# Operands of a TensorE-bound encoder layer, moved by 64 to 128 bytes within a partition

## The chip, the cores and the metric

The kernel runs on one core of a Trainium2 chip. The metric is the device time of one execution in microseconds (us), as the median of several runs. The profile is one further execution.

## The reference

One layer of an encoder block is applied to two requests, of 256 and of 512 tokens, with the same weights; the model width is 1024. Cut to what matters:

```python
h = rmsnorm(x, norm_mix_g)
u, q, k, v, qm, gl = split(h @ w_in)
s5_out   = z * sigmoid(z @ s5_w_glu)          # z = gelu(scan of u, both directions)
diff_out = diff_attention(q, k, v)            # 8 heads, two softmax maps each
mem_out  = memory_attention(qm, rmsnorm(mem)) # 4 heads, 256 memory tokens
br       = [s5_out, diff_out, mem_out] @ w_branch
merged   = sum(sigmoid(gl + b_gate) * br)
x        = x + merged @ w_out
g, up    = split(rmsnorm(x) @ w_gate_up)      # 2 x 2816 columns
x        = x + (silu(g) * up) @ w_down
```

## The kernel before

The two requests are laid side by side as 768 tokens, in two segments (`SEGS`) of 256 and 512. Activations are held feature-major, as tiles of 128 partitions by 8 blocks by 768 tokens.

Each float32 operand is split into a rounded high part and the rest, both of type fp32r, and each product of two operands is three products on TensorE (`mm3`, L755): high by high, high by low, low by high. These three are the lines L756, L757 and L758 of the profile.

```python
def mm3(ps, wh, wl, xh, xl, start, stop):
    pe.matmul(ps, wh, xh, start=start, stop=False)
    pe.matmul(ps, wh, xl, start=False, stop=False)
    pe.matmul(ps, wl, xh, start=False, stop=stop)
```

The first operand of a product is stationary (the weights of TensorE), the second streams. Two helpers call `mm3` over 8 blocks of contraction. `dense_fm` (L760) keeps a weight of the network stationary and streams a segment of an activation, so 256 or 512 columns; `dense_tm` (L766) keeps 128 tokens of an activation stationary and streams columns of the network's weight. In the page's names `gl<-Hhi,wh` the streamed operand stands first.

The order of the work: memory attention (tiles mk, mv, mq, ms, mo), the scan's input (u), the gates (gl, interleaved with the scan), query and key (qk), values (v) and the attention of the eight heads, the branch on the memory attention (br on xm), the half-GLU (glu on z), the branches on the scan (br on s5o) and on the attention (br on xd), the output projection (wo, on mgd), and the FFN. `WStream` loads every weight of the network in order through three buffers, splits it on ScalarE and VectorE (or by DMA) and keeps four pairs of parts ahead.

The FFN goes over the 2816 columns in 11 blocks of 256. The first block multiplies f directly (`first`); each of the ten later ones (`block`, L1389) uses a scheme with seven products of halves instead of eight, 384 columns wide, whose right factors are parts of f (B11, B12 and so on) and the sums T1, T2, T3 in a pool `ffT`; T4 is written over B12. Then `down` (L1423) multiplies the hidden part, tile hid in pool `ffh`, stationary, by two blocks of `w_down`, 512 columns at a time. For `w_down` the first of the two blocks lies in extra tiles (`W.extra`, pools `wxh` and `wxl`), the second in the ordinary ones.

Tiles live in pools that are opened and closed like a stack, from the low end of the partition ("left") or from its high end ("right"). One right-hand pool H holds the normalised input; when it is closed, pool XA takes its place and holds xm, then s5o, then mgd. On the left, pool XB holds z, then xd, then f; after it come x1 (the residual), the FFN's pools, the extra weight tiles, `wsum`, `ffT` and `ffh`. These addresses are fixed when the program is built.

Of the kernel before, what the change touches and what calls it, by code (L numbers as in the profile page):

```python
# [8 lines left out]
F32 = mybir.dt.float32  # L9
# [619 lines left out]
def hybrid_block(ctx, tc, A, outs, consts):  # L629
# [20 lines left out]
    def uid(s):  # L650
        cnt[0] += 1
        return f"{s}_{cnt[0]}"
# [74 lines left out]
            W.add(cols("w_gate_up", 256 * fb + (DFF if what == "up" else 0)), 8, 256, "w" if fb else None)  # L727


    def rsqrt(x, n, tag, bufs=4):  # L730

        i = sm.tile([128, n], I32, name=uid("rqi"), tag=f"rqi{n}")
        y = sm.tile([128, n], F32, name=uid("rqy"), tag=tag, bufs=bufs)
        t = sm.tile([128, n], F32, name=uid("rqt"), tag=f"rqt{n}")
        v.tensor_scalar(out=i, in0=x.bitcast(I32), scalar1=1, scalar2=None, op0=ALU.logical_shift_right)
        v.tensor_scalar(out=y.bitcast(I32), in0=i, scalar1=-1.0, scalar2=float(0x5F3759DF), op0=mul, op1=add)
        for _ in range(3):
            v.tensor_tensor(out=t, in0=y, in1=y, op=mul)
            v.scalar_tensor_tensor(out=t, in0=t, scalar=-0.5, in1=x, op0=mul, op1=mul)
            v.scalar_tensor_tensor(out=y, in0=t, scalar=1.5, in1=y, op0=add, op1=mul)  # L740
        return y
# [78 lines left out]


    hctx, qctx, mctx = ExitStack(), ExitStack(), ExitStack()
    hp_ = hctx.enter_context(tc.tile_pool(name="H", bufs=1, side="right"))
    H = tuple(hp_.tile([128, 8, TOK], F32R, name=f"H{w}") for w in ("hi", "lo"))
    k1 = qctx.enter_context(tc.tile_pool(name="ma1", bufs=1, side="right"))
# [13 lines left out]
    def mem_units(h):  # L839
# [11 lines left out]
        w = W.get()  # L851
        mean_eps(ss, 4, 256)
        rs = rsqrt(ss, 4, "krs")
        for tt in range(4):
            v.scalar_tensor_tensor(out=kr[:, tt], in0=kr[:, tt], scalar=rs[:, tt : tt + 1], in1=gk,
# [32 lines left out]
    def mem_attend():  # L888

        for h in range(4):  # L890
# [9 lines left out]
            qs = sm.tile([128, TILES], F32, name=uid("qs"), tag="qs")  # L900
            v.tensor_scalar(out=qs, in0=ps[:, 0:TILES], scalar1=1.0 / 256, scalar2=1e-6, op0=mul, op1=add)
            rq = rsqrt(qs, TILES, "rq")
            yield
            P, PT = {}, {}
# [51 lines left out]
    with tc.tile_pool(name="nrm", bufs=1) as pool, tc.tile_pool(name="nrmg", bufs=1) as pg:  # L956
# [10 lines left out]
        for tt in range(4):  # L967
# [5 lines left out]
            square_sum(xm[tt], pool, mss[:, tt : tt + 1])  # L973
        mean_eps(mss, 4, 1024)
        v.tensor_copy(mrs, rsqrt(mss, 4, "krs"))
        g = bcast_load(pg, A["norm_mix_g"][0], 1024, "gmix")
        xr = [load_rows(pool, xs[tt]) for tt in range(TILES)]
# [95 lines left out]
    x1ctx, dctx, wctx = ExitStack(), ExitStack(), ExitStack()  # L1073
# [362 lines left out]
    with ExitStack() as c5:  # L1436
# [6 lines left out]
        def pair(pool, nm):  # L1443
            return tuple(pool.tile([128, 8, TOK], F32R, name=uid(nm + w), tag="X" + w) for w in ("hi", "lo"))
# [29 lines left out]
        def load_pair(X, src, scale=None, more=()):  # L1474
            for m in range(8):
                p = zst if m in more else stg
                r = p.tile([128, TOK], F32, name=uid("brr"), tag="brr")
                gp.dma_start(r, src[m])
                split_evac(X[0][:, m], X[1][:, m], r, scale)
# [8 lines left out]
        def tail(c):  # L1488
            if c != 3:
                return  # L1490
            dat.drain()
            dctx.close()
            L["XB"] = x1ctx.enter_context(tc.tile_pool(name="XB", bufs=1))
            Z = L["Z"] = pair(L["XB"], "z")
            load_pair(Z, z_scr, 0.5, (2, 3, 4, 7))
            zctx.close()
            xp = x1ctx.enter_context(tc.tile_pool(name="x1", bufs=1))
            L["x1"] = [xp.tile([128, 1024], F32, name=f"x1_{t}") for t in range(TILES)]

        branch(2, Xm, first=True, tick=dat.tick, hook=tail)  # L1500
        x1, XB, Z = L["x1"], L["XB"], L["Z"]
        S = pair(XA, "s5o")
# [27 lines left out]
        c6 = ctx.enter_context(ExitStack())  # L1530
# [56 lines left out]

    W.extra = tuple(c6.enter_context(tc.tile_pool(name="wx" + w, bufs=1)) for w in "hl")
    W.sums = c6.enter_context(tc.tile_pool(name="wsum", bufs=3))
    tp = c6.enter_context(tc.tile_pool(name="ffT", bufs=1))  # L1590
    fh = c6.enter_context(tc.tile_pool(name="ffh", bufs=1))

    B = {f"B{k}{t}": tuple(x[:, 4 * k - 4 : 4 * k, HT * t - HT : HT * t] for x in F)
# [102 lines left out]
```

## Time and profile before

| | us |
|---|---|
| median of 3 runs | 1806.25 (1805.45 to 1807.45) |
| the profiled execution | 1807.31 |
| its span | 1805.5 |
| PE busy (products) | 1773.6 |
| PEld busy (weight loads, beside the products) | 1629.6 |
| DVE, ACT, POOL busy | 1287.0, 881.7, 278.9 |

The span runs from the first to the last instruction that the profiler saw; the time of the execution is 1.8 us longer. A product's record in the profile is longer than the distance to the start of the next, since products are pipelined; what PE spends on one is read from start to start.

### The profile page before, as it was taken

What the parts mean: (1) busy time and instruction counts of PE and PEld (TensorE: products, weight loads), DVE (VectorE), ACT (ScalarE), POOL (GpSimd) and SP (SyncE); (2) the same over time, 40 slices, a digit from 0 to 9 for tenths busy, and PEclk for the clock granted to TensorE, in tenths of its full rate; (3) what the DMA queues carried; (4) which work ended last, traced back from release to release, by engine and by line L of the source; (5) the groups of instructions that cost most, each with busy time, mean ns of one, the idle gap of its engine ahead of it and who ended that gap; (6) DMA issues with size and microseconds to landing.
All of it is one profiled execution on the core that took longest, in us unless ns stands there. A gap on an engine that the chain in (4) does not pass through costs nothing.

```text
span 1805.5 us, 29484 instructions
## 1 busy us (share of the span) xinstructions
PE 1773.6 (98%) x11286; PEld 1629.6 (90%) x11286; DVE 1287.0 (71%) x2375; ACT 881.7 (49%) x1852; POOL 278.9 (15%) x300
## 2 busy tenths in 40 slices
PE   7999999999999999999989999999999999999999
PEld 7999988999999999999969888888889999999997
DVE  6555758799999568778875535442689777777775
ACT  7444544777676357777656434232333333333331
POOL 0000000000000101111020101000115333333330
PEclk9999999999999999999999999999999999999999
DMA  8422646564655587443373535322302222222221
GB/s 264 128 93 96 112 130 164 145 150 124 155 144 151 143 194 189 112 112 89 88 216 105 199 119 177 105 100 82 82 24 94 71 70 71 71 71 71 71 70 70
DMA packets 192300, 213.12 MB, mean 118 GB/s; under 512 B 58144, under 2 KB 161824, under 8 KB 192160
## 3 DMA queue, kind: packets, MB, share of 16 engines
q1 hardware_dynamic: 174656, 147.27, 27.1%
q0 software_dynamic: 16352, 60.83, 14.5%
q10 hardware_dynamic: 1152, 3.15, 0.5%
q8 instruction: 89, 1.46, 0.3%
q14 instruction: 51, 0.42, 0.1%
HBM read 146.11 MB, written 32.57 MB: 99 GB/s over the span
## 4 chain that ended last, share of the span: by engine, by line
PE 56%; DVE 5%; DMA 4%; ACT 2%; issue 1%; SPq 1%; POOL 0%; ACTq 0%; DVEq 0%; POOLq 0%
PE br L757 4%; PE br L758 4%; PE br L756 4%; PE dn L756 3%; PE dn L757 3%; PE dn L758 3%; PE gate L756 3%; PE gate L757 3%; PE gate L758 3%; PE up L756 3%; PE up L758 3%; PE up L757 3%; PE av L1261 2%; PE qk L758 2%; PE qk L757 2%; PE qk L756 2%
## 5 line engine op out<-in xcount | busy, mean ns | idle before, releaser
L597 ACT ACTIVATE wh<-wr 128x1024 fp32r<-128x1024 f32 x146 | 164.4, 1127 | 98.8 <-DMA wr<-in_w_down_dram 20.1
L603 DVE TENSOR_TENSOR wl<-wr,wh 128x1024 fp32r<-128x1024 f32 x90 | 118.8, 1320 | 91.8 <-ACT wh L597 91.5
L601 POOL DMA_DIRECT2D wl<-wr x56 | 48.9, 873 | 562.3 <-ACT wl L600 466.5
L756 PE MATMUL gl<-Hhi,wh 128*128 128x256 f32 (+1 forms) x384 | 133.1, 347 | 0.8 <-ACT glt L1065 0.8
L757 PE MATMUL gl<-Hlo,wh 128*128 128x256 f32 (+1 forms) x384 | 129.9, 338 | 0.0
L758 PE MATMUL gl<-Hhi,wl 128*128 128x256 f32 (+1 forms) x384 | 129.8, 338 | 0.0
L1431 DVE TENSOR_TENSOR x<-x,dn 128x512 f32<-128x512 f32 x132 | 88.9, 685 | 57.2 <-PE dn L758 57.1
L756 PE MATMUL qk<-wh,Hhi 128*128 128x256 f32 x384 | 108.8, 283 | 1.1 <-ACT qksq L1131 1.1
L757 PE MATMUL qk<-wl,Hhi 128*128 128x256 f32 x384 | 108.7, 283 | 0.0
L758 PE MATMUL qk<-wh,Hlo 128*128 128x256 f32 x384 | 108.6, 283 | 0.0
L559 ACT ACTIVATE wh_S<-ws 128x512 fp32r<-128x512 f32 x70 | 41.7, 623 | 130.5 <-PE dn L758 103.8
L756 PE MATMUL dn<-wh,hidh 128*128 128x512 f32 x264 | 102.4, 390 | 1.2 <-DVE x L1431 1.0
L757 PE MATMUL dn<-wl,hidh 128*128 128x512 f32 x264 | 102.9, 390 | 0.0
L758 PE MATMUL dn<-wh,hidl 128*128 128x512 f32 x264 | 100.8, 390 | 0.0
L756 PEld LDWEIGHTS gl<-Hhi,wh 128*128 128x128 f32 x384 | 72.4, 188 | 8.7 <-ACT glt L1065 1.0
L758 PEld LDWEIGHTS gl<-Hhi,wl 128*128 128x128 f32 x384 | 72.3, 188 | 8.7
L757 PEld LDWEIGHTS gl<-Hlo,wh 128*128 128x128 f32 x384 | 72.4, 188 | 7.8
L756 PEld LDWEIGHTS qk<-wh,Hhi 128*128 128x128 f32 x384 | 72.9, 190 | 2.0 <-ACT qksq L1131 1.3
L758 PEld LDWEIGHTS qk<-wh,Hlo 128*128 128x128 f32 x384 | 73.1, 190 | 0.6
L757 PEld LDWEIGHTS qk<-wl,Hhi 128*128 128x128 f32 x384 | 72.9, 190 | 0.6
L1230 DVE TENSOR_REDUCE nm<-sc 128x1 f32<-128x512 f32 (+1 forms) x96 | 56.8, 597 | 22.5 <-PE sc L1225 21.6
L1232 ACT ACTIVATE p<-sc,nm 128x512 f32<-128x512 f32 (+1 forms) x96 | 59.0, 618 | 24.6 <-DVE nm L1230 20.1
(455 smaller groups left out, 5954.0 us busy)
## 6 DMA issues: line engine op xcount, KB each, us to landing
wl<-wr POOLq DMA_DIRECT2D x56, 512.0 KB, 5.2
wr<-in_w_in_dram SPq DMA_DIRECT2D x48, 512.0 KB, 4.7
wr<-in_w_gate_up_dram SPq DMA_DIRECT2D x44, 512.0 KB, 3.4
wr<-in_w_branch_dram SPq DMA_DIRECT2D x24, 512.0 KB, 4.1
wr<-in_w_down_dram SPq DMA_DIRECT2D x22, 512.0 KB, 3.8
glr<-gl_scr POOLq DMA_DIRECT2D x24, 384.0 KB, 3.4
wr<-in_w_mem_kv_dram SPq DMA_DIRECT2D x16, 512.0 KB, 5.1
wr<-in_w_in_dram SPq DMA_DIRECT2D x32, 256.0 KB, 4.3
```

What stands on the lines that cost most here:

```text
L559: self.nc.scalar.activation(f(hi), src, AF.Copy)
L597: self.nc.scalar.activation(hi, r, AF.Copy)
L601: self.nc.gpsimd.dma_start(lo, r.bitcast(F32R), accum_op=ALU.add)
L603: self.sub.tensor_tensor(out=lo, in0=r, in1=hi.bitcast(F32), op=ALU.subtract)
L756: pe.matmul(ps, wh, xh, start=start, stop=False)
L757: pe.matmul(ps, wh, xl, start=False, stop=False)
L758: pe.matmul(ps, wl, xh, start=False, stop=stop)
L1230: v.tensor_reduce(out=nm[:, m : m + 1], in_=ps, axis=AX.X, op=ALU.max, negate=True)
L1232: act.activation(pm[:, 0:n], ps, AF.Exp, bias=nm[:, m : m + 1], accum_out=s1s[:, tt : tt + 1] if m == 0 else s2)
L1261: pe.matmul(po[:, 0:128], aT[:, 128 * k : 128 * k + 128], V[:, c0 // 128 + k, 128 * (h % 2) : 128 * (h % 2) + 128], start=(k == 0), stop=( ...
L1431: v.tensor_tensor(out=o, in0=o, in1=ps, op=add)
```

## The change

A helper opens a pool with one tile of `n` bytes per partition that nothing uses, so that the pools that are opened after it on the same side start `n` bytes further in. It is called four times: 96 bytes on the right ahead of H, 64 on the left ahead of XB, and 128 each ahead of `ffT` and of `ffh`.

```diff
+    def offset(c, side, n):
+
+        p = c.enter_context(tc.tile_pool(name=uid("offset"), bufs=1, side=side))
+        p.tile([128, n // 4], F32, name=uid("pad"))
...
     hctx, qctx, mctx = ExitStack(), ExitStack(), ExitStack()
+    offset(ctx, "right", 96)
     hp_ = hctx.enter_context(tc.tile_pool(name="H", bufs=1, side="right"))
...
             dctx.close()
+            offset(x1ctx, "left", 64)
             L["XB"] = x1ctx.enter_context(tc.tile_pool(name="XB", bufs=1))
...
     W.sums = c6.enter_context(tc.tile_pool(name="wsum", bufs=3))
+    offset(c6, "left", 128)
     tp = c6.enter_context(tc.tile_pool(name="ffT", bufs=1))
+    offset(c6, "left", 128)
     fh = c6.enter_context(tc.tile_pool(name="ffh", bufs=1))
```

Each engine has the same instructions in the same order, with the same waits, before and after. What differs is where the tiles start in the partition:

| tiles (pool) | start before | start after | modulo 256, before | after |
|---|---|---|---|---|
| weights' parts wh, wl (`whi`, `wlo`) | 25856 and up | the same | 0 | 0 |
| H; later xm, s5o, mgd (`H`, `XA`) | 180192 | 180096 | 224 | 128 |
| memT, kT, V of the memory (`ma0`, `ma2`) | 106432 and up | 96 less | 192 | 96 |
| z, xd, f (`XB`) | 67840 | 67904 | 0 | 64 |
| extra weight tiles (`wxh`, `wxl`) | 151808 and up | 64 more | 0 | 64 |
| T1, T2, T3 (`ffT`) | 166144 and up | 192 more | 0 | 192 |
| hid (`ffh`) | 203008 | 203328 | 0 | 64 |
| attention's tiles (`da1`, `da2`), the scan's (`s5p`, `s5q`) | | the same | | |

Within a tile, parts lie at multiples of 512 bytes from its start, so that the start fixes the remainder for all of them.

## The prediction

> **What bounds the kernel.** I read the head of the page first, then the waits of PE, then the busy time of every engine by stage, and last some stretches in which PE does one kind of product and nothing else.
>
> ```profile
> span 1805.5 us, 29484 instructions
> PE 1773.6 (98%) x11286; PEld 1629.6 (90%) x11286; DVE 1287.0 (71%) x2375; ACT 881.7 (49%) x1852; POOL 278.9 (15%) x300
> ...
> PEclk9999999999999999999999999999999999999999
> ```
>
> PE is busy for 98% of the span at a full clock (a 9 stands for 90% or more). What PE waits for is small; these are the longest rows of its waits, and the whole list is 23 rows long and falls to 0.2 us.
>
> ```profile
> PE qkT L1177 <- DVE qst L1187: 3.9, 2, 2.9
> PE mv L756 <- ACT kr L847: 3.3, 2, 2.0
> PE nT L785 <- DVE memTlo L750: 1.9, 1, 1.9
> ```
>
> By stage (the second number behind the stretch is PE's busy time):
>
> ```profile
> core 0: us, PE busy (x) PEld busy (x) DVE busy (x) ACT busy (x) POOL busy (x), PEclk, DMA share, GB/s
> 7.92:301.67 293.75, 286.02 (x2003) 263.39 (x2003) 186.60 (x526) 152.10 (x286) 8.37 (x35) 1.00 0.50 132
> 301.67:616.15 314.48, 313.72 (x2156) 287.48 (x2154) 281.94 (x387) 212.54 (x489) 23.98 (x29) 1.00 0.58 149
> 616.15:1018.75 402.60, 389.07 (x2953) 368.79 (x2952) 290.26 (x719) 260.78 (x671) 46.20 (x71) 0.99 0.53 137
> 1018.75:1288.69 269.94, 269.94 (x1457) 232.58 (x1456) 121.72 (x176) 85.63 (x118) 20.47 (x39) 1.00 0.38 125
> ...
> 1389.61:1799.10 409.49, 409.28 (x2139) 380.91 (x2139) 314.53 (x443) 126.86 (x221) 146.05 (x101) 1.00 0.21 68
> ```
>
> From 1018.75 to the end PE practically never stops, and no other engine is near its length (DVE 314.53 of 409.49 us in the FFN). So a nanosecond on each product goes into the time one for one, and so does a nanosecond off it, until DVE is the bound, which is 95 us away in the FFN.
>
> **What a product costs, by width and by phase.** The change moves no instruction; it moves addresses. I call the start of an operand modulo 256 bytes its phase; the table in the section on the kernel lists the phases. PE reads two operands at once: the streamed (moving) one of a product, and the weights (stationary) of the next. What matters here is the time from start to start. The stretches below run from the first start of a run of one kind to the start of what follows, so length over number of products is the price. The count in brackets also holds one or two tails of products that began earlier (a record is longer than the spacing); I divide by the products that start inside: 24 in a segment (8 contraction blocks of 3 products), and the number named otherwise.
>
> ```profile
> core 0: us, PE busy (x), PEclk, DMA share, GB/s
> 77.03:79.75 2.72, 2.72 (x26) 1.00 0.00 0
> 103.15:105.68 2.53, 2.53 (x14) 1.00 0.04 13
> 117.79:123.44 5.65, 5.65 (x49) 1.00 0.59 186
> 301.67:304.51 2.84, 2.84 (x25) 1.00 0.78 150
> 324.21:329.81 5.60, 5.60 (x27) 1.00 0.98 204
> 722.37:727.20 4.83, 4.83 (x43) 1.00 0.68 134
> 1130.55:1136.15 5.60, 5.60 (x27) 1.00 0.22 73
> 1144.59:1147.43 2.84, 2.84 (x25) 1.00 0.00 0
> 1189.25:1194.72 5.47, 5.47 (x27) 1.00 0.56 185
> 1211.40:1214.27 2.87, 2.87 (x25) 1.00 0.00 0
> 1219.75:1278.54 58.79, 58.79 (x253) 1.00 0.20 63
> 1389.61:1405.97 16.36, 16.36 (x73) 1.00 0.03 10
> 1405.97:1435.12 29.15, 29.15 (x170) 1.00 0.35 109
> ```
>
> In order: *mk*, 256 wide, streams w (phase 0) against memT (192): 2.72/24 = 113.3 ns. *mo*, 512 wide, pT (0) against Vh (192): 2.53/11 = 230.0. *mk* again, same phases: 5.65/48 = 117.7. *gl*, 256, H (224) against w (0): 118.3; *gl*, 512: 5.60/24 = 233.3. *qk*, 256, w (0) against H (224): 4.83/41 = 117.8. *br* on s5o (224): 512 wide 233.3, 256 wide 118.3. *br* on xd (0): 512 wide 5.47/24 = 227.9, 256 wide 2.87/24 = 119.6. *wo*, 512, w (0) against mgd (224): 58.79/252 = 233.3. *dn*, 512, both 0: 16.36/72 = 227.2. *gate* and *up*, 384, both 0: 29.15/168 = 173.5.
>
> The pair s5o and xd is the best evidence that addresses matter: the same helper, shapes and clock, and 5.4 ns between them at 512 columns. Is it the phase or the region? xd lies low in the partition, s5o at its top. But *dn* has its weights (hid) at the top too, with phase 0, and costs 227.2; *wo* has its weights there with phase 224 and costs 233.3. So it follows the phase, not the place: at 512 columns one operand that starts 32 bytes off a multiple of 64 costs 5.4 to 6.1 ns. At 256 columns it is the other way round: equal phases cost 119.6, 224 costs 117.8 to 118.3, and 192 costs 113.3 or 117.7, so the same addresses have two prices there.
>
> **A rule against it.** Two prices at one width, one clock and one helper, 227.9 and 233.3, are what this trace shows. The Trainium skill, "SBUF — State Buffer", section "Specifications (TRN2)", gives 16-byte cachelines with a penalty each time a read crosses into a new line. All phases here and all shifts are multiples of 16, so by that rule no product crosses more lines or fewer after the change, and the time would stay at 1806. The Trainium skill, "TensorE: Matmul & The Clock Gate", section "Back-to-back issue gap", gives an isolated gap of N/2.4 + 2.5 ns in which no address occurs; by it 512 columns would take 215.8 ns, an estimate, before and after. The trace agrees with neither: every 512 row lies above that, and the rows differ by phase. What the two would make of the time stands below as the rival "nothing".
>
> **The change, part by part.** After it H, s5o, xm and mgd start at phase 128; z, xd, f, hid, x1 and the extra weight tiles at 64; T1 to T3 at 192; memT, kTh, Vh at 96; the ordinary weights stay at 0. No row has a pair 128 apart, so each term has two ends.
>
> (a) 512 wide with H, xm, s5o or mgd: *gl* 24 segments, *mq*, *u*, *br* on xm and on s5o 8 each, so 56 × 24 = 1344, and *wo* 2 × 6 × 24 = 288: 1632 products at 233.3. They come onto a multiple of 64. Ends: 227.9 (as if phases were equal) and 233.3 (as now); between them lies *mo* at 230.0, 64 apart. I take 228.9, the middle of the two multiples of 64 that are on record: −4.4 × 1632 = **−7.2 us** (ends −8.8 and 0).
>
> (b) 256 wide with H, xm or s5o streamed: again 1344, at 118.3; with H as weights: *qk* 8 × 144 = 1152 and *v* 4 × 144 = 576, 1728 in all, at 117.8. Ends: 113.3 and 119.6. I take 117.7, the commoner price of 64 apart: −0.6 × 1344 − 0.1 × 1728 = **−1.0 us** (ends: −5.0 × 1344 − 4.5 × 1728 = −14.5, and +1.3 × 1344 + 1.8 × 1728 = +4.9).
>
> (c) z, xd and the first FFN block on f, from 0 to 64 apart: 480 products of 512 (*glu* 192, *br* 192, *gate* and *up* 96), 227.9 to 228.9, and 480 of 256, 119.6 to 117.7: +0.5 − 0.9 = **−0.4 us** (ends −3.0, with 256 at 113.3, and +2.6, with 512 at 233.3 and 256 as it is).
>
> (d) *gate* and *up* of the ten later blocks, 20 × 84 = 1680 products of 384, from 0 to 64 (f) or 192 (T) apart. No row has this width off phase. At 256 columns, 64 apart is 1.9 to 6.3 cheaper than equal phases; at 512 it is 2.1 dearer; 384 lies midway, so I take **0**. Ends: 384/256 × 113.3 = 170.0 (an estimate from *mk*) gives −5.9, and the penalty of 5.4 that 512 has gives +9.1.
>
> (e) *dn*, 11 × 72 = 792 at 227.2. Its left tile comes from the extra pool (64) for one contraction block, so 396 stay at equal phases and 396 go 192 apart: +1.0 × 396 = **+0.4 us** (ends 0 and +2.4 at 233.3).
>
> (f) memT goes from 64 apart to 160, now 32 bytes off: *mk* and *mv*, 768 products, between 113.3 and 117.7 now, 117.8 after, the price of the nearest 32-byte-off row. The two *mk* rows together come to (48 × 117.7 + 24 × 113.3)/72 = 116.2: +1.6 × 768 = **+1.2 us** (ends 0 and +3.5). *mo* and *ms* are under 250 products; I leave them at 0.
>
> (g) ScalarE, VectorE and DMA on moved tiles: taken at nothing, hidden behind PE. If the cover went, PE's waits above show where; the largest is 3.9 us in all.
>
> Sum: −7.2 − 1.0 − 0.4 + 0 + 0.4 + 1.2 = **−7.0 us**. The profiled execution took 1807.3 us, so 1800.3 by itself; it is 1.1 above the median of 1806.25, from which the same sum gives **1799.2**.
>
> **Rivals.** *The FFN loses what it has* (slower). At 512 the cheapest rows are those of equal phase, *dn*'s 227.2 and xd's 227.9, and the change takes equal phase away from (c), half of (e) and all of (d), while (a) gets a distance of 128 that is equal to nothing. If only equal phase is cheap, (a) gains 0, (d) costs 9.1, (c) 2.6 and (e) 2.4: +14.1, 1820. It decides once 384-wide products rise by more than (a) falls: about 4.3 ns a product for 7.2 us. For it: no 512 row off phase is as low as 227.9. Against it: at 256 equal phase is the dearest.
>
> *All pairs come free* (faster by more). *mk*'s 113.3 at 256 and *dn*'s 227.2 at 512 are both 0.44 ns a column, which may be the price with no collision at all. If every pair 64, 128 or 192 apart gets it, (a) −8.8, (b) −14.5, (c) −3.0, (d) −5.9: −32, 1774. Against it: *mk* itself has 117.7 as often, and *mo* 230.0 at the same distance.
>
> *Nothing* (gains and losses that cancel): if 128 apart behaves as equal phase, (a) gives −8.8 and (b) takes back 4.9; with (e) at +2.4 and (f) at +1.2 only −0.3 is left, 1806. The two rules of the Trainium skill quoted above end at the same time.
>
> **How the numbers follow.** What a measurement can tell from no change here is 0.2%, 3.6 us. The sum's own case, 1793 to 1802.6: 0.48. All pairs free, below 1793: 0.14; a part of the pairs is enough for that. Nothing, within 3.6 us: 0.13. The FFN's loss: 0.25. Faster 0.62, same 0.13, slower 0.25. The range goes down to 1785, two thirds of the way to the free case, and up to 1816, seven tenths of the way to the FFN's loss; I put about 0.08 below it and 0.12 above.
>
> **What would show it.** In the profile after, the same stretches, shifted: *gl* and *wo* at 512 columns near 229 instead of 233.3 confirm (a); *qk* near 117.7 confirms (b); the FFN's 84 products at 173.5 confirm (d), at 178 the slower rival, at 170 the free one. One period of the FFN (two runs of 84 and one of 72) is 45.51 us now, the 29.15 and the 16.36 above. I am wrong if *gl* stays at 233.3, or if a distance of 128 costs more than 224 did: this trace has no row that excludes it.

## The result, and the profile after

The changed kernel is slower. Its median is 1814.41 us (6 runs, 1812.38 to 1815.84) against 1807.78 us of the kernel before (6 runs, the three of the section "Time and profile before" among them): the ratio is 1.0038, 95% interval [1.0027, 1.0049], or 4.9 to 8.9 us. The profiled execution took 1812.95 us, 5.6 us more than the one of before. Its head:

```profile
span 1811.2 us, 29484 instructions
...
PE 1781.6 (98%) x11286; PEld 1634.1 (90%) x11286; DVE 1286.3 (71%) x2375; ACT 881.4 (49%) x1852; POOL 278.5 (15%) x300
```

The instructions are the same in number. PE's busy time has grown by 8.0 us, DVE's and ACT's have not. The stages that the prediction showed, in the kernel after (stretch, length, PE busy and so on):

```profile
7.67:302.22 294.55, 287.77 (x2002) 265.19 (x2003) 186.28 (x526) 151.57 (x286) 8.36 (x35) 1.00 0.50 132
302.22:617.19 314.97, 313.80 (x2155) 287.75 (x2154) 281.90 (x387) 212.44 (x489) 24.00 (x29) 1.00 0.59 148
617.19:1020.98 403.79, 390.41 (x2953) 370.17 (x2952) 290.19 (x719) 260.99 (x671) 46.19 (x71) 0.99 0.53 137
1020.98:1290.64 269.66, 269.66 (x1457) 232.02 (x1456) 121.73 (x176) 85.64 (x118) 20.47 (x39) 1.00 0.39 125
1290.64:1391.44 100.80, 98.19 (x549) 89.73 (x548) 88.43 (x123) 41.56 (x68) 33.08 (x21) 1.00 0.27 77
1391.44:1806.85 415.41, 415.20 (x2148) 383.24 (x2148) 315.79 (x445) 126.78 (x221) 145.68 (x101) 1.00 0.22 68
```

The last stage runs here to the start of the last product; in the kernel before, the same stretch is

```profile
1389.61:1801.22 411.61, 411.40 (x2149) 382.64 (x2148) 316.10 (x445) 126.86 (x221) 146.05 (x101) 1.00 0.21 68
```

So the FFN's later blocks lost 3.8 us and the first three stages 0.8, 0.5 and 1.2; the two between gained 0.3 and 0.1. And the same thirteen stretches of one kind of product each, in the same order as in the prediction (*mk*; *mo*; *mk*; *gl* 256; *gl* 512; *qk*; s5o 512; s5o 256; xd 512; xd 256; *wo*; *dn*; *gate* and *up* 384):

```profile
76.35:79.19 2.84, 2.84 (x27) 1.00 0.00 0
102.79:105.35 2.56, 2.56 (x13) 1.00 0.06 18
117.45:123.15 5.70, 5.70 (x50) 1.00 0.60 184
302.22:305.10 2.88, 2.88 (x25) 1.00 0.80 152
325.18:330.78 5.60, 5.60 (x27) 1.00 1.00 205
723.19:728.05 4.86, 4.86 (x42) 1.00 0.75 148
1132.56:1138.16 5.60, 5.60 (x26) 1.00 0.24 73
1146.60:1149.47 2.87, 2.87 (x25) 1.00 0.00 0
1191.21:1196.71 5.50, 5.50 (x26) 1.00 0.62 200
1213.38:1216.21 2.83, 2.83 (x25) 1.00 0.00 0
1221.72:1280.52 58.80, 58.80 (x254) 1.00 0.21 63
1391.44:1408.13 16.69, 16.69 (x74) 1.00 0.03 11
1408.13:1437.35 29.22, 29.22 (x169) 1.00 0.35 109
```

Read them against those of before. *gl* at 512 columns takes 5.60 us for 24 products as before, s5o 5.60 as before, *wo* 58.80 instead of 58.79: 128 bytes off the weights' phase costs what 224 bytes off cost. *dn* went from 16.36 to 16.69 for 72 products, and with eleven such runs that is 3.6 us, over half of the loss of 5.7 us that the span shows.

### The profile page after: what moved, and what is told of

Read it like the earlier page. It is cut to its first block, busy times and chain, and to the rows that moved or that the text cites. A ratio compares the mean times of both kernels' runs of the same rounds, so it can differ in the third digit from the quotient of the medians.

```text
span 1811.2 us, 29484 instructions
## 1 busy us (share of the span) xinstructions
PE 1781.6 (98%) x11286; PEld 1634.1 (90%) x11286; DVE 1286.3 (71%) x2375; ACT 881.4 (49%) x1852; POOL 278.5 (15%) x300
## 4 chain that ended last, share of the span: by engine, by line
PE 58%; DVE 4%; DMA 4%; ACT 1%; issue 1%; POOL 0%; SPq 0%; ACTq 0%; DVEq 0%; POOLq 0%
PE br L762 4%; PE br L763 4%; PE br L761 4%; PE dn L761 3%; PE dn L762 3%; PE dn L763 3%; PE gate L761 3%; PE gate L762 3%; PE gate L763 3%; PE up L761 3%; PE up L762 3%; PE up L763 3%; PE av L1267 2%; PE qk L762 2%; PE qk L763 2%; PE qk L761 2%
## 5 line engine op out<-in xcount | busy, mean ns | idle before, releaser
L603 DVE TENSOR_TENSOR wl<-wr,wh 128x1024 fp32r<-128x1024 f32 x90 | 118.3, 1314 | 93.5 <-ACT wh L597 92.7
```

What stands on the lines that cost most here:

```text
L603: self.sub.tensor_tensor(out=lo, in0=r, in1=hi.bitcast(F32), op=ALU.subtract)
```

## The experiments

All of them move addresses alone: the instructions, their order and their waits are those of the kernel before. The theory under test is that the price of a product depends on the distance, modulo 256 bytes, between the start of the operand that streams and the start of the weights, and on the width. The distance is counted as the streamed operand's phase minus the weights'. Its rivals are that an operand's own phase counts (a multiple of 64 is good), or its place in the partition.

**Every tile on the left moved together (left64).**

```diff
+    lp0 = ctx.enter_context(tc.tile_pool(name="offset0", bufs=1))
+    lp0.tile([128, 16], F32, name="pad0")
     W = WStream(nc, tc, ctx)
```

> One pad of 64 bytes ahead of the weight buffers moves every tile on the left, the weights' parts included, to phase 64; the right side stays at 224 and 192. Pairs that had equal phases keep them (64 and 64). If the distance between the two operands sets the price: dn stays at 227.2 ns, gate and up at 173.5, glu and br on xd at 227.9 and 119.6; only pairs with the right side move (H against the weights from 224 to 160 apart, memT from 64 to 128 apart), which by the changed kernel's rows costs 0 to 3 us. If the phase of an operand by itself sets the price: dn goes to about 230 as the half with both at 64 had in the changed kernel (+2 us) or to 233 (+4.7 us), and the 384-wide products to 174.7 or more (+2 us and up).

Measured: ratio 1.0044 [1.0032, 1.0057], 5.8 to 10.3 us slower. The stretches of *qk*, *dn* and of *gate* with *up*:

```profile
728.88:733.80 4.92, 4.92 (x42) 1.00 0.70 132
...
1398.15:1414.51 16.36, 16.36 (x73) 1.00 0.03 11
1414.51:1443.66 29.15, 29.15 (x170) 1.00 0.36 109
```

*dn* with both operands at 64 costs 16.36 us, to the digit what it cost with both at 0, and so do the 384-wide products (29.15). The phase of an operand by itself does not count; the distance does. The time by itself looks like the rival's; it is these rows that exclude it. The distance theory missed the time too (it expected 0 to 3 us), because the right side came to distances that no earlier row had: *qk*, now 96 apart, costs 4.92/41 = 120.0 ns here instead of 117.8. Averaged over all products of a kind in the trace (how is said below the table), *qk* and *v* rise from 117.0 to 119.7, which is 4.6 us on 1728 products; *mk* and *mv*, 128 apart, add 1.5, and the products of 512 columns with H, xm or s5o streamed, now 160 apart, about 1.3. Together that is 7.4 us, close to what the medians differ by (7.7).

**The right-hand part alone (r96).**

```diff
+    offset(ctx, "right", 96)
     hp_ = hctx.enter_context(tc.tile_pool(name="H", bufs=1, side="right"))
```

> The right-hand part of the change alone (96 bytes ahead of H, so H, xm, s5o and mgd at 128, memory tiles at 96). By the distance theory, with the rows of the changed kernel: 512 wide unchanged (233), 256 wide with H as weights 117.0 to 118.7, memory 116.6 to 118.1, so slower by 1.7 to 4.4 us, the FFN as before (dn 227.2). By the theory that all of the loss is the FFN's: no change within 0.5 us.

Measured: ratio 1.0012 [1.0003, 1.0020], 0.5 to 3.6 us slower, as the distance theory had it; the other theory's bound of 0.5 us is only just excluded. *gl* 256 and 512, s5o 256, *wo* and *dn*:

```profile
303.23:306.10 2.87, 2.87 (x25) 1.00 0.79 151
326.03:331.63 5.60, 5.60 (x26) 1.00 0.99 204
...
1149.23:1152.11 2.88, 2.88 (x26) 1.00 0.00 0
1224.41:1282.97 58.56, 58.56 (x253) 1.00 0.21 63
1394.04:1410.40 16.36, 16.36 (x74) 1.00 0.03 9
```

This part gains nothing at 512 columns (*wo* falls by 0.2 us in all) and loses some at 256. The FFN is untouched.

**hid and the extra weight tiles alone (dn64).**

```diff
+    offset(c6, "left", 64)
     W.extra = tuple(c6.enter_context(tc.tile_pool(name="wx" + w, bufs=1)) for w in "hl")
     W.sums = c6.enter_context(tc.tile_pool(name="wsum", bufs=3))
+    offset(c6, "left", 192)
     tp = c6.enter_context(tc.tile_pool(name="ffT", bufs=1))
+    offset(c6, "left", 64)
     fh = c6.enter_context(tc.tile_pool(name="ffh", bufs=1))
```

> Only hid and the extra weight tiles go to phase 64, as in the changed kernel; H, XB and T keep the phases they had. By the distance theory dn goes from 227.2 to about 231.7, as in the changed kernel (half of it 192 apart, half at equal phases but in alternation with the other half): slower by 3 to 3.6 us, which is over half of the whole loss. gate and up stay at 173.5. By the rival that dn became dearer because other tiles (x1, f, T) moved as well: less than 1 us.

Measured: ratio 1.0024 [1.0015, 1.0033], 2.7 to 6.0 us slower, so about as expected. *dn*:

```profile
1392.09:1408.76 16.67, 16.67 (x73) 1.00 0.03 11
```

16.67/72 = 231.5 ns, almost the price in the changed kernel (231.8), with x1, f and T where they were.

**hid alone (hid64).**

```diff
+    offset(c6, "left", 64)
     fh = c6.enter_context(tc.tile_pool(name="ffh", bufs=1))
```

> Only hid goes to 64; the extra weight tiles stay at 0, so all of dn has its operands 192 apart. Distance theory: all 792 products at about 233, +4.6 us. If the half of dn with equal phases was dear in the changed kernel only because it alternates with the other half, the whole is then twice the dear half and no more; if a run of one distance is cheaper than alternation, dn comes out at 230 or below, +2 us.

Measured: ratio 1.0022 [1.0013, 1.0030], 2.4 to 5.4 us slower. *dn*, all of it 192 apart:

```profile
1389.00:1405.80 16.80, 16.80 (x73) 1.00 0.04 12
```

16.80/72 = 233.3. A uniform distance of 192 is not cheap either. And if half at 192 and half at equal phases cost the mean, dn64 would have shown (233.3 + 227.2)/2 = 230.3; it showed 231.5. The single products show where the rest comes from: in dn64 the half with equal phases takes 229.8 ns on average, against 227.5 for the same half in the kernel before, and the half 192 apart 233.2. So the half with equal phases lost a part of its low price where three products of it alternate with three of the other.

**z, xd, f and x1 alone (xb64).**

```diff
+            offset(x1ctx, "left", 64)
             L["XB"] = x1ctx.enter_context(tc.tile_pool(name="XB", bufs=1))
...
+    offset(c6, "left", 192)
     W.extra = tuple(c6.enter_context(tc.tile_pool(name="wx" + w, bufs=1)) for w in "hl")
```

> Only z, xd, f, x1 and two small FFN pools go to 64; extra weights, T and hid are put back to phase 0. By the distance theory, with the rows of the changed kernel: 512 wide on z, xd, f 227.9 to 229.1, 256 wide 119.5 to 117.4, 384 wide on f 173.5 to 173.4, dn at 227.2: faster by 0.3 to 0.8 us. By the rival that the residual x1 or the FFN's small pools cost something when moved: slower.

Measured: ratio 0.9998 [0.9989, 1.0007]. The expected 0.3 to 0.8 us is below what these runs can tell. The rows agree with it: xd 512 and 256, and the 384-wide products with f at 64 and T at 0:

```profile
1188.96:1194.45 5.49, 5.49 (x26) 1.00 0.62 202
1211.09:1213.92 2.83, 2.83 (x26) 1.00 0.00 0
...
1405.46:1434.63 29.17, 29.17 (x170) 1.00 0.35 109
```

5.49/24 = 228.8 and 2.83/24 = 117.9: 64 apart is a little dearer than equal phases at 512 and cheaper at 256.

**H at other distances: 0, 64 and 192 (r224, r160, r32).** The pad ahead of H is 224, 160 or 32 bytes. For the first two, room comes from spare buffers that no instruction waits on; with these gone the tiles on the left start 256 bytes lower, so that their phases stay:

```diff
-            ss = sm.tile([128, t1 - t0], F32, name=uid("xss"), tag=f"xss{t1 - t0}")
+            ss = sm.tile([128, t1 - t0], F32, name=uid("xss"), tag=f"xss{t1 - t0}", bufs=1)
...
-            rs = rsqrt(ss, t1 - t0, "xrs")
+            rs = rsqrt(ss, t1 - t0, "xrs", 2)
```

> 224 bytes ahead of H instead of 96, nothing on the left, so H, xm, s5o and mgd start at 0 like the weights (memory tiles at 224). Room for it comes from buffers of four one- or two-use scalars; instructions and waits are the same. Distance theory: 512 wide with these tiles 233.2 to 227.5 (1632 products, -9.3 us), 256 wide streamed 118.3 to 119.6 (+1.7), as weights 117.0 to 119.5 (+4.3): faster by about 3 us. The theory that each operand only has to start on a multiple of 64: as with 96 bytes, 233 and 118.7, so slower by 2 us. The theory that the upper end of the partition is the dear one: no change.

Measured: ratio 0.9981 [0.9972, 0.9989], 2.0 to 5.1 us faster. *gl* 256 and 512, *qk*, s5o 256, *wo*:

```profile
299.99:302.86 2.87, 2.87 (x25) 1.00 0.71 140
323.04:328.51 5.47, 5.47 (x26) 1.00 0.98 204
720.76:725.67 4.91, 4.91 (x42) 1.00 0.69 136
1144.27:1147.14 2.87, 2.87 (x26) 1.00 0.00 0
1219.33:1276.45 57.12, 57.12 (x253) 1.00 0.20 65
```

> 160 bytes ahead of H: H, xm, s5o, mgd at 64, memory at 32. Distance theory, with the rows of z and xd at 64: 512 wide streamed 233.1 to 229.1 (1344 products, -5.4 us), 256 wide streamed 118.3 to 117.5 (-1.1), wo (weights 192 behind the streamed) stays at 233, as weights at 256 wide near 117: faster by 5 to 7 us. Multiples-of-64 theory: as with 96 bytes, slower by 2 us.

Measured: ratio 0.9968 [0.9956, 0.9981], 3.4 to 8.0 us faster. The same five:

```profile
300.40:303.12 2.72, 2.72 (x25) 1.00 0.73 145
323.26:328.77 5.51, 5.51 (x27) 1.00 0.98 203
720.32:724.98 4.66, 4.66 (x43) 1.00 0.63 124
1141.00:1143.83 2.83, 2.83 (x26) 1.00 0.00 0
1216.04:1274.84 58.80, 58.80 (x253) 1.00 0.21 63
```

> 32 bytes ahead of H: H, xm, s5o, mgd at 192, memory at 160. Distance theory: 192 apart when streamed has only T's row (384 wide, 174.7, dearer than equal phases) and dn's (233.1): 512 wide stays near 233; 256 wide streamed 116.7 to 118; as weights (64 apart) 116.6; wo (64 apart) 230: faster by 0 to 4 us. Multiples-of-64 theory: like 96 bytes, slower by 2 us.

Measured: ratio 0.9993 [0.9984, 1.0002], at the edge of what can be told. *gl* 256 and 512, *qk*, s5o 256 and *wo*:

```profile
303.17:306.00 2.83, 2.83 (x26) 1.00 0.77 149
326.60:332.19 5.59, 5.59 (x27) 1.00 0.98 202
724.34:729.17 4.83, 4.83 (x42) 1.00 0.67 133
1147.20:1149.92 2.72, 2.72 (x25) 1.00 0.00 0
1222.24:1279.93 57.69, 57.69 (x254) 1.00 0.20 64
```

The three and r96 move the same tiles to four multiples of 64. The time goes from 1.2 thousandths above to 3.2 below, so a multiple of 64 is not what counts; and H's upper end of the partition is as cheap as any, 57.12/252 = 226.7 ns for *wo* with the weights there. In r224, H and the weights start an odd multiple of 256 bytes apart, in the kernel before xd and the weights an even one, and both pairs cost 227.9 at 512 columns: a step of 256 bytes makes no difference there. In ns from start to start, worked out from the rows above and those of the prediction (the entries marked "mean" are explained below):

| distance | 0 | 32 | 64 | 128 | 192 | 224 |
|---|---|---|---|---|---|---|
| 512 columns | 226.7 to 227.9 | 233.3 | 228.8 to 230.0 | 232.4 to 233.3 | 232.9 to 233.3 | 233.3 |
| 384 columns, mean | 173.3 to 174.0 | | 173.2 to 173.4 | | 174.7 | |
| 256, H as weights | 119.8 | 117.8 | 117.8 | 118.5 | 113.7 | |
| the same, mean | 119.5 | 117.0 | 117.1 | 118.7 | 115.1 to 115.7 | |
| 256, H or s5o streamed | 119.6 | | 113.3 to 117.9 | 119.6 to 120.0 | 113.3 to 117.9 | 118.3 |
| 256, H streamed, mean | 119.5 | | 116.5 to 117.1 | 118.7 | 115.7 | 118.3 |

A stretch is one sample. The means are taken over all products of a kind in a run's trace (*qk* and *v*; *gl*, *u* and *mq*; *gate* and *up*), from each start to the next; distances in time above 150 ns at 256 columns, 200 at 384 and 270 at 512, in which PE waited or went on to other work, are left out. At 512 columns the means lie within 1 ns of the stretches. At 256 columns they do not: at 64 and at 192 most stretches have one of two prices, and the distance sets how often they have which. Of 23 stretches of *gl*, 6 cost about 113.5 ns and 17 about 118 at 64 apart (r160); at 192 apart (r32) 16 cost about 114 and 7 about 118. What decides for a stretch is not known. So at 256 columns one stretch is no price.

**Distances chosen by that table (chosen).** H and the memory's tiles at 64, xm, s5o and mgd at 0, z, xd, f and T at 64, hid and the extra weight tiles at 0. The spare buffers are freed as above.

```diff
+    offset(ctx, "right", 160)
     hp_ = hctx.enter_context(tc.tile_pool(name="H", bufs=1, side="right"))
...
+    offset(qctx, "right", 224)
     k2 = qctx.enter_context(tc.tile_pool(name="ma2", bufs=2, side="right"))
...
+        offset(c5, "right", 64)
         XA = c5.enter_context(tc.tile_pool(name="XA", bufs=1, side="right"))
...
+            offset(x1ctx, "left", 64)
             L["XB"] = x1ctx.enter_context(tc.tile_pool(name="XB", bufs=1))
...
+    offset(c6, "left", 192)
     W.extra = tuple(c6.enter_context(tc.tile_pool(name="wx" + w, bufs=1)) for w in "hl")
     W.sums = c6.enter_context(tc.tile_pool(name="wsum", bufs=3))
+    offset(c6, "left", 64)
     tp = c6.enter_context(tc.tile_pool(name="ffT", bufs=1))
+    offset(c6, "left", 192)
     fh = c6.enter_context(tc.tile_pool(name="ffh", bufs=1))
```

> Offsets chosen from the measured prices by distance: H and the memory tiles at 64, xm, s5o and mgd at 0, z, xd, f and T at 64, hid and the extra weight tiles at 0 (weights at 0 throughout); same instructions and waits. By the distance theory, from the steady parts of the runs with 160 and 224 bytes: gl, mq, u, qk, v -7.6 us, br on xm and s5o and wo -3.1, XB and T -0.7, memory -0.9: 12 us less of PE's time, of which waits may take some back, so 1796 to 1799 against 1808. By the theory that the gains of 160 and 224 bytes were of another kind (the region of a tile, or chance): no better than 160 bytes alone, 1802.

Measured: 1796.32 us against 1807.0, ratio 0.9940 [0.9926, 0.9954]: 8.3 to 13.4 us faster, and beyond r160, so the prices add up over the parts. *mk* (48 products), *gl* 512, *qk*, s5o 512, *wo*, *dn*, and *gate* with *up* (384 columns, f and T both 64 apart):

```profile
117.07:122.53 5.46, 5.46 (x49) 1.00 0.67 192
...
322.65:328.16 5.51, 5.51 (x27) 1.00 0.99 203
718.82:723.48 4.66, 4.66 (x43) 1.00 0.64 127
1124.59:1130.05 5.46, 5.46 (x26) 1.00 0.26 75
...
1212.56:1269.71 57.15, 57.15 (x253) 1.00 0.21 65
1380.46:1396.79 16.33, 16.33 (x73) 1.00 0.04 12
1396.79:1425.91 29.12, 29.12 (x169) 1.00 0.35 109
```

## Why the prediction was wrong

The frame held: PE is the bound, nothing but addresses moved, and the price follows phases and not places. The 1814.41 lies inside the range, but that is the range's width and not the mechanism: I forecast a gain of 7 us and gave 0.62 to faster.

**The step that failed is the choice of a value between the two ends for pairs 128 apart, in (a).** I took 228.9, "the middle of the two multiples of 64 that are on record", as though every multiple of 64 were of one kind. Behind it stands the reading that an operand "that starts 32 bytes off a multiple of 64" pays. *gl* and *wo* at 128 show 233.3, the dear end, so (a) is 0 instead of −7.2 us. r160 and r224 show what would have been right: the gain that I saw was there, at distances of 64 and 0 (229.6 and 227.9), and the change went to neither.

(b) has the wrong sign: *gl* 256 went from 118.3 to 120.0 and s5o 256 from 118.3 to 119.6, a mean of 1.5 on 1344 products, and *qk* from 117.8 to 118.5 on 1728: +3.2 us by these rows instead of −1.0. The end that I had named was +4.9. The means give +3.4 us, but split otherwise: with H, xm or s5o streamed the price rose by 0.4 (0.5 us), with H as weights from 117.0 to 118.7 (2.9 us). So the 117.8 that the prediction took for *qk* was one dear stretch, and that the rows come to nearly the same sum is luck.

(c) was right: xd rose by 1.3 at 512 and fell by 1.7 at 256, −0.2 us against −0.4.

(d) was nearly right: 0.07 us more in 168 products, 0.7 us in the ten blocks, against 0. By the means the products on T, 192 apart, rose from 173.3 to 174.7, and those on f, 64 apart, fell by 0.2. The wide bounds were not needed.

(e) was mis-sized: +3.6 us (0.33 × 11) instead of +0.4. I gave products 192 apart the price of 64 apart and left the equal half at its low price. 192 costs 233.3 (hid64), and the equal half rises where it alternates with the other (dn64).

(f) came out as 8.54 us in place of 8.37 for the two *mk* stretches, 2.4 ns on 768 products, +1.8 us against +1.2. By the means it is 1.5 ns and +1.2 us, as forecast; *mo* and *ms*, left at 0, added 0.7.

These rows sum to 0 + 3.2 − 0.2 + 0.7 + 3.6 + 1.8 = +9.1 us, the means over the kernel to +8.7 with *mo* and *ms*; the span grew by 5.7. The stages show where the difference lies. From 1018.75 on, where PE practically never stops, the means come to 3.8 us and the stages grew by 3.4. In the first three stages the means come to 4.9 and the stages grew by 2.5. In those PE also waits: what its record leaves idle there, length less busy time, is 22.0 us before and 21.3 after, and a short pause does not count as idle in it, since a record is longer than the distance to the next start (about 280 ns against 118 at 256 columns). That a dearer product eats into a wait that another engine sets would explain the rest; it was not followed wait by wait.

The slower rival named the right place for the wrong reason. It had the FFN lose equal phase and priced 384 columns at +9.1 us; they took 0.7, while *dn* alone took 3.6 and the 256-wide products with H as weights most of the rest. "Nothing", with 128 behaving as equal phase, is excluded by r224 against r96: 5.47 and 5.60 for the same 24 products. With it the two rules of the Trainium skill that I had set beside it ("SBUF — State Buffer", "Specifications (TRN2)", and "TensorE: Matmul & The Clock Gate", "Back-to-back issue gap") fail here: neither lets a shift by a multiple of 16 bytes change the price, and pads alone moved the whole time from 1.0038 to 0.9940 of the kernel before. "All pairs free" fails on the same rows.

## What to carry to other kernels

Where TensorE is the bound with fp32r operands, read the price of a product from start to start, group it by width and by the distance between the two operands' addresses, and fill the table by moving one pool at a time before choosing pads: here the good distances at 512 columns were 0 and 64, and at 256 columns 192, then 64. Average over every product of a kind before trusting a price: at 256 columns single stretches differed by over 4 ns at one distance. A value between two known distances is not an estimate for a third. A pad ahead of one pool moves every pool behind it, so list all pairs that change before counting the one that should gain.

## What the runs showed of the hardware that was not expected

The price depends on the sign of the distance: 64 and 192 are the same step either way, yet at 512 columns they cost 229 and 233, and at 256, with H as weights, 117.1 (r32) and 115.7 (r160) on average. Equal phases are the cheapest at 512 (227) and among the dearest at 256 (119.5). The price also depends on the products around: the half of *dn* with equal phases took 229.8 instead of 227.5 in alternation with the other (dn64). And one pair of addresses can have two prices: *mk* ran at 113.3 and at 117.7 in the kernel before, and why is open. What collides, and in which unit, these runs do not show. They show that the price goes by the distance between the two operands (left64); whether the weights that count are those of the running product or of the next was not tried, since in these runs both mostly have one phase.
